# Last down product and last token block in two parts of 172 and 86 columns; factors of the other blocks by a product with ones

## The chip, the core and the metric

The kernel runs on one core of a Trainium2 chip. The metric is the device time of one execution in microseconds (us). Engines are named as the profile names them: PE is TensorE (PEld its weight loads), DVE VectorE, ACT ScalarE, POOL GpSimd, SP SyncE, which issues most DMAs.

## What is computed

One decoder layer on 1024 prompt tokens and 8 sample tokens, 1032 columns in all, model width 1024. The change touches the end of it: the channel mixer's down projection, its residual addition, and the final RMSNorm.

```python
def rmsnorm(x, g):
    xf = x.astype(jnp.float32)
    y = xf * lax.rsqrt(jnp.mean(xf * xf, axis=-1, keepdims=True) + EPS)
    return (y * g.astype(jnp.float32)).astype(x.dtype)

def sq_relu_mlp(h, w_up, w_down):
    return jnp.square(jax.nn.relu(h @ w_up)) @ w_down
...
        xp = xp + sq_relu_mlp(rmsnorm(xp, norm_mlp[l]), w_up[l], w_down[l])
...
    y_prompt = rmsnorm(xp, norm_final)
    y_sample = rmsnorm(xd, norm_final)
```

## The kernel before

Activations lie transposed: features on the 128 partitions, tokens in columns. The 1032 columns are two halves of 516, each of two chunks of QC = 258; QCOLS[2 * c + half] is a block of 258 columns. A f32 product is made of three single-pass products on values split into a high and a low part in the type fp32r (UH and UL, wh and wl), which accumulate in one PSUM bank.

The down projection is done with seven block products (Strassen's scheme, `q` in 1, 2, 6, 7, 4, 5, 3) in four groups `g` of the hidden width. A step (q, p, c) is one call of `lower`: 12 products of 128x128 weights and 258 columns for the feature tile `p` and the chunk `c`; then DVE adds the bank to the accumulator `c` of its quadrant (line 2413). The accumulators hold the residual as well. TensorE's order is pinned to the program's (`pinned`); the other engines' order is set by the tile framework's scheduler.

In the last part of group 3 (`end`), q is 5 and then 3, and the steps go chunk by chunk: n = 0 to 7 for c = 0, n = 8 to 15 for c = 1. With each addition of q 4, 2, 5 and 3 go the squares for the final norm (`squares`): ACT squares the 258 columns, DVE or POOL adds them into `ssf`; the square of the last tile of a chunk (`sqt`) is kept apart (`tails`).

The final norm of a block takes two steps, at the places that COLUMNS_AT and ROWS_AT give. `finish_columns` calls `factor_columns`: for each 86 columns (QP) of the block a product with the sums of squares as weights and a column of ones gives the sum over partitions as one column; the tail is a second term; ACT takes the square root, DVE the reciprocal (`fc`, 86x3). ACT also multiplies the accumulators by the norm's gain (line 2334). `finish_rows` calls `factor_rows`: for each 86 columns a product with the broadcast factor as weights and the identity writes the factors as a row on all partitions; DVE multiplies the accumulators by it (line 2342), and SP, for the last block ACT too, issues the output. The last block, (c, half) = (1, 1), does both after n = 15, in four multiplications of two feature tiles each.

`ones` is a 128x1 column and `onesq` a 128x128 square of ones, both f32; `factor_columns` and `factor_rows` serve the norm before the up projection as well (`norm_factor`, `norm_rows`).

Of the kernel before, what the change touches and what calls it, by code (L numbers as in the profile page):

```python
# [48 lines left out]
def decoder_step(ctx: ExitStack, tc: tile.TileContext, i: dict, o: dict):  # L49
# [1929 lines left out]
    def factor_columns(bank, sums, last, x):  # L1979
        col = bank[:QP, 300:303]  # L1980

        terms = [(y, j) for y in (sums, last) if y is not None for j in range(3)]
        for n, (y, j) in enumerate(terms):
            pinned(nc.tensor.matmul(
                col[:, j : j + 1], y[:, j * QP : j * QP + QP], ones[:, :1], start=n == 0, stop=n >= len(terms) - 3,
                skip_group_check=True))
        fc = KC.tile([QP, 3], F32, tag=f"fc{x % 2}", name=f"fc_{x}", bufs=2)
# [4 lines left out]
    def factor_rows(bank, fc):  # L1992
        for j in range(3):
            mm(bank[:, j * QP : j * QP + QP], fc[:, j : j + 1].to_broadcast([QP, P]), ident[:QP, :QP], True, True)
        return bank[:, :QC]
# [3 lines left out]
    def norm_factor(x):  # L1999
        fp = PD.tile([P, 512], F32, tag=("mk", "dt")[x % 2], name=f"rm_{x}", bufs=1)  # L2000
        FACTORS[x] = fp, factor_columns(fp, ssum[:, QCOLS[x]], None, x)
# [239 lines left out]
    with pool("acc", side="right") as AC, pool("rd", side="right") as RD, pool("w") as A, pool("w_ps", space=PSUM) as PS:  # L2241
# [22 lines left out]
        COLUMNS_AT, ROWS_AT, tails = {0: (0, 0), 3: (1, 0), 10: (0, 1), 15: (1, 1)}, {2: (0, 0), 5: (1, 0), 12: (0, 1), 15: (1, 1)}, {}  # L2264
# [39 lines left out]
        def lower(w, s, c, ps, first):  # L2304
            cq = slice(c * QC, c * QC + QC)
            for k in range(4):
                wk, wkl = w[:, k * P : k * P + P], w[:, 512 + k * P : 512 + k * P + P]
                for x, (l, r) in enumerate(((wk, s[0]), (wk, s[1]), (wkl, s[0]))):
                    pinned(nc.tensor.matmul(  # L2309
                        ps, l, r[:, k, cq], start=first and k == 0 and x == 0, stop=k == 3 and x == 2, skip_group_check=True))  # L2310

        def squares(quad, p, c, tail=False):
            cs = QCOLS[2 * c + HALF_OF[quad]]
            x = C[quad][:, p, c * QC : c * QC + QC]
# [11 lines left out]
        ends = {}  # L2326

        def finish_columns(c, half):
            fp = PS.tile([P, 512], F32, tag=f"acc{turns[0] % 8}", name=f"fin_{c}_{half}", bufs=1)
            turns[0] += 1  # L2330
            ends[c, half] = fp, factor_columns(fp, ssf[:, QCOLS[2 * c + half]], tails[c] if half else None, 4 + 2 * c + half)
# [3 lines left out]

        def finish_rows(c, half):
            cs = QCOLS[2 * c + half]
            rf = factor_rows(*ends[c, half])
            n = 2 if (c, half) == (1, 1) else 4
            for ft in range(0, 8, n):  # L2340
                y = C[((11, 21), (12, 22))[half][ft // 4]][:, ft % 4 : ft % 4 + n, c * QC : c * QC + QC]
# [285 lines left out]
```

## Time and profile before

| | |
|---|---|
| median of 3 runs | 1488.96 us (1487.69 to 1489.63) |
| the profiled execution | 1496.69 us |
| its span, first to last instruction | 1494.8 us, mean granted clock 0.995 |
| PE, PEld busy | 98%, 94% of the span |
| DVE, ACT, POOL busy | 73%, 45%, 21% |

All durations of rows come from the one profiled execution; times in them count from the span's start. An engine's busy share is an average over stages with different limits. The chain that ended last is followed back from the last instruction: at each step to what released it, or to the instruction before it on its engine.

### The profile page before, as it was taken

The numbers are of one execution on the slowest core, as the hardware profiler recorded it, in microseconds if no ns is written. First come the engines' busy times: TensorE is split into PE (matmuls) and PEld (weight loads), VectorE is DVE, ScalarE is ACT, GpSimd is POOL, SyncE is SP. The second block draws the span as 40 slices with busy tenths as digits, with TensorE's granted clock in tenths as the row PEclk, the third lists the DMA queues.
The fourth block names the chain that finished last, engine by engine and source line by source line (L and its number), as shares of the span: only waits on it lengthen the run. The fifth ranks groups of instructions, "written<-read, shape, count | busy, mean of one in ns | idle before, by whom it ended". The sixth has DMA issues, their size and how long they took to land.

```text
span 1494.8 us, 27880 instructions
## 1 busy us (share of the span) xinstructions
PE 1471.7 (98%) x10925; PEld 1401.8 (94%) x10925; DVE 1098.7 (73%) x2264; ACT 679.6 (45%) x1325; POOL 321.1 (21%) x346
## 2 busy tenths in 40 slices
PE   9999999998999999999999999999999999999997
PEld 7899779998779999989999999999999999999997
DVE  7666436887767636567886988888888879787865
ACT  7543435665552431248535643434334443343454
POOL 0035323123414311105022100000001311110380
PEclk9999999999999999999999999999999999999998
DMA  8255728213847157474582444344436774536273
GB/s 287 65 185 180 202 58 189 71 47 110 268 145 283 59 195 175 145 228 102 178 304 68 136 148 145 128 154 157 156 139 209 239 251 142 171 101 198 72 128 114
DMA packets 125238, 236.69 MB, mean 158 GB/s; under 512 B 13748, under 2 KB 76521, under 8 KB 124978
## 3 DMA queue, kind: packets, MB, share of 16 engines
q1 hardware_dynamic: 89064, 170.51, 36.0%
q0 software_dynamic: 24912, 44.80, 11.0%
q10 hardware_dynamic: 11130, 19.60, 3.5%
q8 instruction: 86, 1.41, 0.4%
q14 instruction: 46, 0.38, 0.1%
HBM read 170.25 MB, written 57.52 MB: 152 GB/s over the span
## 4 chain that ended last, share of the span: by engine, by line
PE 84%; DVE 8%; ACT 3%; issue 2%; DMA 2%; POOL 0%; ACTq 0%; another core or an unknown queue 0%; SPq 0%; DVEq 0%; POOLq 0%
PE dn L2309 19%; PE Z L2143 9%; PE qkp L75 7%; PE mq L75 6%; PE Y L2143 6%; PE X L2143 6%; PE pr_o L75 6%; PE pr_m L75 4%; PE grp L75 3%; PE sp L75 2%; PE av L75 2%; PE mv L75 1%; PE mk L75 1%; PE mpv L75 1%; PE vap_z L522 1%
## 5 line engine op out<-in xcount | busy, mean ns | idle before, releaser
L2309 PE MATMUL dn<-UH,wd 128*128 128x258 f32 x1792 | 325.1, 283 | 0.8 <-DVE c L2413 0.3
L2309 PEld LDWEIGHTS dn<-UH,wd 128*128 128x128 f32 x1792 | 277.6, 189 | 1.8 <-issue 0.8
L2309 PE MATMUL dn<-UL,wd 128*128 128x258 f32 x896 | 252.7, 282 | 0.0
L2309 PEld LDWEIGHTS dn<-UL,wd 128*128 128x128 f32 x896 | 169.0, 189 | 0.0
L2413 DVE TENSOR_TENSOR c<-c,dn 128x258 f32<-128x258 f32 x216 | 88.5, 417 | 38.2 <-PE dn L2309 35.8
L2169 ACT ACTIVATE hq<-r 128x258 f32<-128x258 f32 x128 | 53.9, 422 | 114.1 <-DVE r L2168 114.1
L2143 PE MATMUL X<-UH,wu 128*128 128x258 f32 x512 | 97.4, 282 | 0.9 <-ACT p L2194 0.9
L2143 PE MATMUL Z<-T_h,wu 128*128 128x258 f32 x512 | 98.2, 284 | 0.0
L2287 ACT CAST wd<-raw_d 128x512 fp32r<-128x512 f32 x96 | 58.8, 620 | 78.4 <-PE dn L2309 73.2
L1953 ACT CAST wu<-raw_up 128x512 fp32r<-128x512 f32 x96 | 59.2, 617 | 62.2 <-PE Z L2143 54.7
L2280 ACT CAST UH<-raw_h 128x1032 fp32r<-128x1032 f32 x56 | 58.8, 1057 | 55.0 <-PE dn L2309 27.3
L2143 PEld LDWEIGHTS X<-UH,wu 128*128 128x128 f32 x512 | 81.3, 188 | 1.1 <-ACT p L2194 1.1
L2143 PEld LDWEIGHTS Z<-T_h,wu 128*128 128x128 f32 x512 | 81.3, 189 | 0.0
L2281 DVE TENSOR_TENSOR UL<-raw_h,UH 128x1032 fp32r<-128x1032 f32 x56 | 73.4, 1311 | 9.9 <-ACT UH L2280 9.9
L2180 POOL DMA_DIRECT2D HT<-ht x32 | 17.2, 536 | 292.4 <-DVE ht L2179 291.9
L2288 DVE TENSOR_TENSOR wd<-raw_d,wd 128x512 fp32r<-128x512 f32 x96 | 72.0, 757 | 10.0 <-ACT wd L2287 9.9
L2143 PE MATMUL Z<-T_l,wu 128*128 128x258 f32 x256 | 72.3, 282 | 0.0
L2143 PE MATMUL X<-UL,wu 128*128 128x258 f32 x256 | 72.3, 282 | 0.0
L128 ACT CAST wh_u<-raw_u 128x1024 fp32r<-128x1024 f32 x43 | 44.7, 1049 | 54.2 <-PE mq L75 31.2
L1954 DVE TENSOR_TENSOR wu<-raw_up,wu 128x512 fp32r<-128x512 f32 x96 | 64.5, 684 | 3.7 <-ACT wu L1953 3.7
L129 DVE TENSOR_TENSOR wl_u<-raw_u,wh_u 128x1024 fp32r<-128x1024 f32 x39 | 51.6, 1328 | 18.3 <-ACT wh_u L128 18.1
L2301 POOL TENSOR_TENSOR raw_d<-raw_d,raw_d 128x512 f32<-128x512 f32 x16 | 22.1, 1382 | 194.5 <-DVE raw_d L2297 173.4
(598 smaller groups left out, 4718.2 us busy)
## 6 DMA issues: line engine op xcount, KB each, us to landing
raw_u<-in_wall SPq DMA_DIRECT2D x49, 512.0 KB
HT<-ht POOLq DMA_DIRECT2D x32, 516.0 KB
raw_h<-HT SPq DMA_DIRECT2D x32, 516.0 KB
raw_up<-in_wall SPq DMA_DIRECT2D x32, 512.0 KB
raw_d<-in_wall SPq DMA_DIRECT2D x32, 512.0 KB
HQ<-hq ACTq DMA_DIRECT2D x32, 387.0 KB
raw_h<-HQ SPq DMA_DIRECT2D x24, 516.0 KB
cmk<-in_cmk SPq DMA_DIRECT2D x16, 512.0 KB
```

The costliest lines, as they stand in the source:

```text
L75: pinned(nc.tensor.matmul(out, l, r, start=start, stop=stop))
L129: (lo_engine or nc.vector).tensor_sub(wl[:, :n], raw[:, :n], wh[:, :n].bitcast(F32))
L1953: nc.scalar.copy(w[:, :512], src)
L1954: nc.vector.tensor_sub(w[:, 512:], src, w[:, :512].bitcast(F32))
L2143: pinned(nc.tensor.matmul(ps, l, r[:, k, :], start=first and k == 0 and x == 0, stop=k == 3 and x == 2, skip_group_check=True))
L2169: nc.scalar.activation(h[:, PLACE[quad], :], r, AF.Square)
L2280: nc.scalar.copy(h, rv)
L2281: nc.vector.tensor_sub(l, rv, h.bitcast(F32))
L2287: nc.scalar.copy(w[:, :512], src)
L2288: nc.vector.tensor_sub(w[:, 512:], src, w[:, :512].bitcast(F32))
L2309: pinned(nc.tensor.matmul(ps, l, r[:, k, cq], start=first and k == 0 and x == 0, stop=k == 3 and x == 2, skip_group_check=True))
L2413: nc.vector.tensor_add(y, y, ps)
```

## The change

For the three earlier blocks the two steps become one, `finish_sums`: a product of the sums with the square of ones gives the sum over partitions on all partitions at once, as 128x258 (block (0, 1) needs two products, the tail's too); ACT takes the square root in PSUM, DVE the reciprocal of 258 columns into `ssf`, and `finish_rows` multiplies by `ssf` without a further product.

The last step (3, 3, 1) and the last block are cut into PARTS, 172 and 86 columns: `lower`, the addition and the square of the tail are done for one part and then for the other. After the loop `final_sums` is done for both parts, then `final_rows` for both. `factor_columns` and `factor_rows` take n = 2 or 1 instead of 3. The last block's multiplications are of four feature tiles and one part each.

```diff
+    def factor_columns(bank, sums, x, last=None):
+        n = sums.shape[-1] // QP
+        col = bank[:QP, 300 : 300 + n]
...
-        COLUMNS_AT, ROWS_AT, tails = {0: (0, 0), 3: (1, 0), 10: (0, 1), 15: (1, 1)}, {2: (0, 0), 5: (1, 0), 12: (0, 1), 15: (1, 1)}, {}
+        SUMS_AT, ROWS_AT, tails = {0: (0, 0), 3: (1, 0), 10: (0, 1)}, {2: (0, 0), 5: (1, 0), 12: (0, 1)}, {}
...
+        WHOLE, PARTS = slice(0, QC), (slice(0, 2 * QP), slice(2 * QP, QC))
+
+        def lower(w, s, c, ps, first, part):
+            cq = slice(c * QC + part.start, c * QC + part.stop)
...
-                sq = A.tile([P, QC], F32, tag="sqt", name=f"sqt_{c}", bufs=2)
+                sq = A.tile([P, QC], F32, tag="sqt", name=f"sqt_{c}_{part.start}", bufs=3)[:, part]
...
+        def finish_sums(c, half):
+            f = acc_bank(f"fin_{c}_{half}")
+            y = ssf[:, QCOLS[2 * c + half]]
+            mm(f, onesq, y, True, not half)
+            if half:
+                mm(f, onesq, tails[c, 0], False, True)
+            nc.scalar.activation(f, f, AF.Sqrt, scale=1.0 / D, bias=epsc)
+            nc.vector.reciprocal(y, f)
             for ft in range(8):
                 y = C[((11, 21), (12, 22))[half][ft // 4]][:, ft % 4, c * QC : c * QC + QC]
                 nc.scalar.activation(y, y, AF.Copy, scale=g_fin[:, ft : ft + 1])
...
+        def final_sums(part):
+            fp = PS.tile([P, 512], F32, tag=f"acc{turns[0] % 8}", name=f"fin_1_1_{part.start}", bufs=1)
+            turns[0] += 1
+            y = ssf[:, QCOLS[3]][:, part]
+            ends[part.start] = fp, factor_columns(fp, y, 4 + part.start, tails[1, part.start])
+            for ft in (3,) if part.start else (0, 1, 2, 3, 4, 5, 6, 7):
+                y = final_y(ft, 1, part if ft == 3 else WHOLE)
+                nc.scalar.activation(y, y, AF.Copy, scale=g_fin[:, ft : ft + 1])
+
+        def final_rows(part):
+            rf = factor_rows(*ends[part.start])
+            cs = slice(HALF + QC + part.start, HALF + QC + part.stop)
+            for ft in (4, 0):
+                y = final_y(ft, 4, part)
+                nc.vector.tensor_mul(y, y, rf.unsqueeze(1).to_broadcast([P, 4, part.stop - part.start]))
+                (nc.scalar if ft else nc.sync).dma_start(
+                    o["yT"][ft * P : (ft + 4) * P, cs].rearrange("(f p) c -> p f c", p=P), y)
...
-                steps = [(q, p, c) for q in qs for p in ps_ for c in range(2)]
+                steps = [(q, p, c, WHOLE) for q in qs for p in ps_ for c in range(2)]
                 if end:
-                    steps = [(q, p, c) for c in range(2) for q in qs for p in ps_]
-                for n, (q, p, c) in enumerate(steps):
+                    steps = [(q, p, c, WHOLE) for c in range(2) for q in qs for p in ps_]
+                    steps[-1:] = [(*steps[-1][:3], x) for x in PARTS]
+                for n, (q, p, c, part) in enumerate(steps):
...
+        for part in PARTS:
+            final_sums(part)
+        for part in PARTS:
+            final_rows(part)
```

The order of instructions at the end of TensorE's queue, before (`fin_1` is the bank of the last block's factors, `dn_5_3_1` that of the last product):

```order
L2309 MATMUL dn_5_3_1_17235<-UH,wd_3_3_17150 128x258 x2
L2309 MATMUL dn_5_3_1_17235<-UL,wd_3_3_17150 128x258
L2309 MATMUL dn_5_3_1_17235<-UH,wd_3_3_17150 128x258
L1984 MATMUL fin_1_17322<-ones,ssumf 86x1 x3
L1984 MATMUL fin_1_17322<-ones,sqt_17320 86x1 x3
L75 MATMUL fin_1_17322<-ident,fc_17329 128x86 x3
```

and in the changed kernel, from the last products of the second part on:

```order
L2313 MATMUL dn_5_3_1_17218<-UH,wd_3_3_17138 128x86 x2
L2313 MATMUL dn_5_3_1_17218<-UL,wd_3_3_17138 128x86
L2313 MATMUL dn_5_3_1_17218<-UH,wd_3_3_17138 128x86
L1985 MATMUL fin_1_0_17317<-ones,ssumf 86x1 x2
L1985 MATMUL fin_1_0_17317<-ones,sqt_0_17300 86x1 x2
L1985 MATMUL fin_1_172_17333<-ones,ssumf 86x1
L1985 MATMUL fin_1_172_17333<-ones,sqt_172_17315 86x1
L75 MATMUL fin_1_0_17317<-ident,fc_17322 128x86 x2
L75 MATMUL fin_1_172_17333<-ident,fc_17336 128x86
```

The column products of both parts stand behind the products of both; the row products of the first part stand behind the columns of the second.

The end of ACT's queue in the changed kernel (`sqt_0` and `sqt_172` are the squares of the two parts' last tile, `c_13388` the accumulators of quadrant 12, features 0 to 511, `c_13387` of quadrant 22, `fc` the factors):

```order
L2321 ACTIVATE sqt_0_17300<-c_13388 128x172
L2354 ACTIVATE c_13388<-c_13388,g_fin 128x172
L1989 ACTIVATE fc_17322<-fin_1_0_17317,epsc 86x2
L2321 ACTIVATE sqt_172_17315<-c_13388 128x86
L2354 ACTIVATE c_13388<-c_13388,g_fin 128x86
L1989 ACTIVATE fc_17336<-fin_1_172_17333,epsc 86x1
L2362 DMA out_yT<-c_13387 128x4x172
L2362 DMA out_yT<-c_13387 128x4x86
```

The square of the second part stands behind the square root of the first part's factors, which reads what TensorE's columns wrote.

The end of DVE's queue in the changed kernel:

```order
L2442 TENSOR_TENSOR c_13388<-c_13388,dn_5_3_1_17218 128x172
L2442 TENSOR_TENSOR c_13388<-c_13388,dn_5_3_1_17218 128x86
L1990 RECIPROCAL fc_17322<-fc_17322 86x2
L2361 TENSOR_TENSOR c_13387<-c_13387,fin_1_0_17317 128x4x172
L1990 RECIPROCAL fc_17336<-fc_17336 86x1
L2361 TENSOR_TENSOR c_13388<-c_13388,fin_1_0_17317 128x4x172
L2361 TENSOR_TENSOR c_13387<-c_13387,fin_1_172_17333 128x4x86
L2361 TENSOR_TENSOR c_13388<-c_13388,fin_1_172_17333 128x4x86
```

The two additions of the last product come first, then one reciprocal for each part and four multiplications of four feature tiles.

## Rows read from the trace of the kernel before

**Rows 1.** The page: busy time of TensorE; shares of the chain that ended last.

```profile
PE 1471.7 (98%) x10925; PEld 1401.8 (94%) x10925; DVE 1098.7 (73%) x2264; ACT 679.6 (45%) x1325; POOL 321.1 (21%) x346
...
PE 84%; DVE 8%; ACT 3%; issue 2%; DMA 2%; POOL 0%; ACTq 0%; another core or an unknown queue 0%; SPq 0%; DVEq 0%; POOLq 0%
```

**Rows 2.** The chain that ended last, from 1456 us: start, us, what.

```profile
1458.44 0.39 PE fin L1984 x6
...
1461.81 0.64 PE fin L75 x6
...
1464.31 2.97 PE dn L2309 x24
...
1467.92 7.24 PE dn L2309 x60
1475.16 0.85 PE fin L1984 x12
...
1478.99 0.65 PE fin L75 x6
...
1482.37 0.34 DVE c L2413
...
1483.72 0.43 DVE ssumf L2324
...
1487.78 0.69 DVE c L2342
```

**Rows 3.** Timeline: start, us, engine, line, operation, count [idle before <-releaser].

```profile
1473.75 0.42 DVE L2413 TENSOR_TENSOR c<-c,dn 128x258 f32<-128x258 f32 x1 [1.00 <-PE dn L2309]
...
1483.70 0.28 PE L2309 MATMUL dn<-UH,wd 128*128 128x258 f32 x1
1484.20 0.62 PE L1984 MATMUL fin<-ones,ssumf 128*86 128x1 f32 x6 [0.22 <-DVE ssumf L2324]
...
1485.64 0.26 ACT L1988 ACTIVATE fc<-fin,epsc 86x3 f32<-86x3 f32 x1 [0.17 <-PE fin L1984]
```

**Rows 4.** Windows: us, busy time (instructions) by engine, PEclk, DMA share, GB/s.

```profile
1484.00:1486.00 2.00, 1.24 (x12) 1.07 (x12) 0.54 (x3) 1.48 (x4) 0.00 (x0) 1.00 0.60 164
1486.00:1488.00 2.00, 1.58 (x6) 1.36 (x6) 0.33 (x2) 0.00 (x0) 0.00 (x0) 0.51 0.03 9
...
1490.00:1492.00 2.00, 0.00 (x0) 0.00 (x0) 0.28 (x1) 0.00 (x0) 0.00 (x0) 0.50 1.03 345
```

**Rows 5.** Timeline of TensorE elsewhere: plain-f32 products in a row.

```profile
146.96 1.10 PE L75 MATMUL sc<-qblk,kT 128*128 128x256 f32 x4
...
324.32 1.84 PE L75 MATMUL ct<-ones,sq 128*128 128x1 f32 x16
...
833.67 1.47 PE L75 MATMUL rm<-ident,fc 86*128 86x86 f32 x12
```

**Rows 6.** Groups by form: out<-in, shapes xcount | busy us, mean ns | idle before.

```profile
L2309 PE MATMUL dn<-UH,wd 128*128 128x258 f32 x1792 | 325.1, 283 | 0.8 <-DVE c L2413 0.3 <-ACT c L2410 0.3
...
L2309 PEld LDWEIGHTS dn<-UH,wd 128*128 128x128 f32 x1792 | 277.6, 189 | 1.8 <-issue 0.8 <-ACT c L2410 0.5 <-DVE c L2413 0.3
...
L545 PEld LDWEIGHTS vrp_d<-wl_vr,UD 128*8 128x8 f32 x16 | 1.4, 88 | 0.0
...
L2342 DVE TENSOR_TENSOR c<-c,fin 128x1032 f32<-128x1032 f32 x6 | 7.3, 1225 | 0.4 <-PE fin L75 0.4
...
L1013 DVE RECIPROCAL mn<-sm 128x1 f32<-128x1 f32 x32 | 5.1, 159 | 2.4 <-ACT e L1006 1.8 <-issue 0.5
...
L1067 DVE RECIPROCAL c<-sm 128x8 f32<-128x8 f32 x4 | 0.8, 188 | 0.0
```

**Rows 7.** DMA queues, 1488 to 1495: packets, MB, share of 16 engines.

```profile
q1 hardware_dynamic: 544, 0.53, 22.7%
q10 hardware_dynamic: 544, 0.53, 22.0%
```

**Rows 8.** The same, 238.1 to 239.0, 512 bytes a packet.

```profile
q1 hardware_dynamic: 432, 0.22, 104.7%
```

More of the change, by code (lines that the diff above doesn't have):

```diff
@@ L1977, in decoder_step @@
     QP = QC // 3
[L1979 to L1983, printed above, removed]
+    def factor_columns(bank, sums, x, last=None):
+        n = sums.shape[-1] // QP
+        col = bank[:QP, 300 : 300 + n]
+        terms = [(y, j) for y in (sums, last) if y is not None for j in range(n)]
+        for m, (y, j) in enumerate(terms):
             pinned(nc.tensor.matmul(
-                col[:, j : j + 1], y[:, j * QP : j * QP + QP], ones[:, :1], start=n == 0, stop=n >= len(terms) - 3,
+                col[:, j : j + 1], y[:, j * QP : j * QP + QP], ones[:, :1], start=m == 0, stop=m >= len(terms) - n,
                 skip_group_check=True))
-        fc = KC.tile([QP, 3], F32, tag=f"fc{x % 2}", name=f"fc_{x}", bufs=2)
+        fc = KC.tile([QP, 3], F32, tag=f"fc{x % 2}", name=f"fc_{x}", bufs=2)[:, :n]
         nc.scalar.activation(fc, col, AF.Sqrt, scale=1.0 / D, bias=epsc[:QP])
@@ L1992, in factor_rows @@
     def factor_rows(bank, fc):
-        for j in range(3):
+        n = fc.shape[-1]
+        for j in range(n):
             mm(bank[:, j * QP : j * QP + QP], fc[:, j : j + 1].to_broadcast([QP, P]), ident[:QP, :QP], True, True)
-        return bank[:, :QC]
+        return bank[:, : n * QP]
     FACTORS = {}
@@ L2334, in finish_columns, with final_y @@
                 nc.scalar.activation(y, y, AF.Copy, scale=g_fin[:, ft : ft + 1])
+        ends = {}
+        def final_y(ft, n, part):
+            return C[(12, 22)[ft // 4]][:, ft % 4 : ft % 4 + n, QC + part.start : QC + part.stop]
+        def final_sums(part):
[14 more added lines that the diff above has]
+                    o["yT"][ft * P : (ft + 4) * P, cs].rearrange("(f p) c -> p f c", p=P), y)
         def finish_rows(c, half):
             cs = QCOLS[2 * c + half]
[L2338 to L2341, printed above, removed]
-                nc.vector.tensor_mul(y, y, rf.unsqueeze(1).to_broadcast([P, n, QC]))
-                (nc.scalar if n == 2 and ft % 4 else nc.sync).dma_start(
-                    o["yT"][ft * P : (ft + n) * P, cs].rearrange("(f p) c -> p f c", p=P), y)
+            rf = ssf[:, cs]
+            for ft in range(0, 8, 4):
+                y = C[((11, 21), (12, 22))[half][ft // 4]][:, ft % 4 : ft % 4 + 4, c * QC : c * QC + QC]
+                nc.vector.tensor_mul(y, y, rf.unsqueeze(1).to_broadcast([P, 4, QC]))
+                nc.sync.dma_start(o["yT"][ft * P : (ft + 4) * P, cs].rearrange("(f p) c -> p f c", p=P), y)
         pin[0] = True
@@ L2419, in decoder_step @@
                         if q in (2, 4, 5, 3):
[L2420 removed]
+                            tail = squares(INTO[q], p, c, (q, p) == (3, 3), part)
                         if tail is not None:
[L2422 to L2424 removed]
+                            tails[c, part.start] = tail
+                        if end and n in SUMS_AT:
+                            finish_sums(*SUMS_AT[n])
                         if end and n in ROWS_AT:
                             finish_rows(*ROWS_AT[n])
+        for part in PARTS:
+            final_sums(part)
+        for part in PARTS:
+            final_rows(part)
         pin[0] = False
```

24 lines of the change are left out of this document (7 added, 17 removed).

## The prediction

> **What bounds the kernel now.** I read the page first. TensorE is busy for 98% of the span and carries 84% of the chain that ended last [rows 1], so an edit on its queue counts while that queue is full. The chain in order of time says until when [rows 2]: from 1458 on it is down products (dn) with small norm products (fin) between them, nothing else; after 1479.64 it passes to VectorE (DVE) and ScalarE (ACT), but TensorE has no idle time before the first fin of the last group, which starts at 1484.20, 0.22 of it waited [rows 3]. From there TensorE is no longer the limit. The end is a relay: last addition, square, column products, square root, reciprocal, row products, multiplications, output transfers [rows 3]. The windows show two more things [rows 4]: the granted clock is 1.00 to 1486 and 0.51 (the 1.2 GHz level) after it, when TensorE had been busy for only 1.24 of the last 2.00 us; and the transfers fill the 16 DMA engines from 1490 to 1492 (share 1.03). So there are two regions: a full TensorE queue up to the last product, and a serial tail of 11 us.
>
> The sum below is made against the profiled execution (1496.69 us, span 1494.8, 1.9 around it). It is 7.7 us above the median of the three runs, 1488.96; I take the same number of us off both.
>
> **TensorE before the last product: 1.9 us less.** In the last group of the loop the three earlier blocks lose their column and row products. The chain gives their share: columns 0.39 twice and 0.85, rows 0.64, 0.63 and 0.65, together 3.55 [rows 2] (of the two 0.39 one stands there, of the rows the first and the last). In their place come four products of 128x258 in plain f32 (one, one, two). None of that shape is in the trace. The nearest is sc, 128x256 in plain f32: four records, two products, in 1.10 us [rows 5], so 0.55 each at most, and about 0.45 where the next product hides the last record's tail. I take 0.47, four are 1.9. That leaves 1.65. Each switch between dn and fin costs besides: 24 dn records between two fin groups take 2.97 [rows 2], 24 at the pitch of 0.12 (60 in 7.24) take 2.88, so 0.1 a switch, and three fin groups fewer are 0.3. Bounds 1.35 and 2.2; I take 1.9. The last product, whose 12th record starts at 1483.70 [rows 3] and whose first therefore started near 1482.38, then begins at 1480.45.
>
> The new square roots (128x258 on ACT, about as long as the addition of that size, 0.42, against 0.26 now [rows 3]) lie in ACT's idle time. The three new reciprocals of 258 columns are DVE work. Small ones take 159 ns for one column and 188 for eight [rows 6], 4 ns a column, so 1.2 us each (below: 0.42 like an addition; above: 2.0, twice the slope less the start). DVE has room between the additions, which wait for products (1.00 ahead of the one at 1473.75 [rows 3]); I count nothing. What covers it is the last product: DVE must only have the first part's addition and ACT its square done before TensorE reaches the columns that read it.
>
> **The last product: 1.25 us more.** 12 products of 258 columns take 12 x 0.12 = 1.44. Now there are 12 of 172 and 12 of 86, each with its own weight load. A load's record grows from 88 ns at 8 columns to 189 at 128 [rows 6], 0.84 ns a column, so 128 columns occupy the loader for about 0.11. The 1-column products of ct, with the same 128 columns of weights and next to nothing to stream, say the same: 16 in 1.84, 0.112 each without the tail [rows 5]. So I take 0.112 for every one of the 24, whatever its columns: 2.69. Below: time by columns alone, 0.12 x 172/258 and 0.12 x 86/258, 1.44 in all. Above: the plain-f32 price, in the rivals. It ends at 1483.15 instead of 1483.82.
>
> **The tail to the first multiplication: 2.15 us earlier.** TensorE's order puts both parts' products ahead of any columns, so the first part's norm does not start under the second part's products; only its addition and square do. Before, the sums stood 1.44 us after the end of the last but one addition (1482.71 to 1484.15) [rows 2]; that addition now ends near 1481.15, so the sums stand by 1482.6, the 172 columns are added by 1482.9 and squared by 1483.25. Their columns are reached at 1483.5, after four others: in time. The first part's eight column records (0.08 each: six take 0.62 with the last one's tail [rows 3]) end at 1483.9, their result at 1484.05. Square root to 1484.31. Now comes what is queued behind what: on ACT the second part's square stands behind this square root, so it ends near 1484.6, and on TensorE the first part's row products stand behind the columns that read that square. These end at 1484.8, so the four row records run to 1485.4 at 0.112 each (rm: 12 in 1.47 at full clock [rows 5]; to 1485.9 at the half clock, where six took 1.58 [rows 4]). The reciprocal is done meanwhile. The first multiplication is now 4x172 columns, between 516 in 0.69 [rows 2] and 1032 in 1.22 [rows 6], so 0.87, and ends at 1486.32; before, the first one ended at 1488.48 [rows 2]. The second part's factors hide under it.
>
> **The output transfers: 0.8 us more.** After the first multiplication the DMA engines set the pace [rows 4]: two queues with 544 packets each, at 22.7% and 22.0% of 16 engines over 7 us [rows 7], are 46 ns a packet, 64 data packets an engine, 3.0 us. Bytes stay the same, packets double: 64 of 688 bytes and 64 of 344 an engine. Below: by bytes, nothing more. Above: the 512-byte packets of [rows 8] take 35 ns (432 at 104.7% of 0.9 us); on that line 688 bytes are 39 and 344 bytes 31, 4.5 us, 1.5 more. I take 0.8. The last multiplication and its issue end near 1488.2, ahead of their turn.
>
> **Sum.** -2.15 + 0.8 = -1.35, rounded -1.4: the profiled execution at 1495.3, the runs at 1487.6, 0.09% faster. With the bounds of these terms (0.3 and 0.55 on TensorE, 0.5 for the half clock, 0.8 and 0.7 on the transfers) 1486.5 to 1489.3. About 0.2% (2.98 us: below 1485.98, above 1491.94) is what a measurement of this kernel can tell from no change.
>
> **Rivals.**
> First, products by columns (0.15). If a weight load hides fully even under 86 columns, the last product stays 1.44 and ends at 1481.9; then the first part's square (1483.25) binds the columns, whose result comes at 1483.75 instead of 1484.05: 0.3 more, 1487.3. Against it stand the ct rows [rows 5]. The Trainium skill ("TensorE: Matmul & The Clock Gate", Back-to-back issue gap) gives columns / 2.4 GHz + 2.5 ns for an isolated gap, 74 and 38 ns here, 1.35 us in all; the trace does not bear that out for loads of 128 f32 columns.
>
> Second, ending slower (0.25): the single-pass products (fp32r, one record each, where a plain f32 product has two) fall to the plain-f32 price. The down products all have 258 columns [rows 6], and no row shows a single-pass product of fewer than 256. Place: the 24 products at the end. Price: rm, 86 columns, 12 records or six products in 1.47, 0.225 each; sc at 256 about 0.45; so 172 near 0.32. 12 x (0.32 + 0.225) = 6.5, 3.8 above the 2.69 taken: -1.4 + 3.8 = +2.4, 1491.4. It decides from 24 products in 4.1 us, 0.17 each. For it: nothing in the trace, but nothing excludes it either. Against it: the load of such a product has the same length as that of a wide one.
>
> Third, the narrow output packets (0.08). The 86-column part writes 344-byte runs. If each costs two moves, 64 x 31 ns come on top: +2.0, +0.6 in all, 1489.6. The Trainium skill ("DMA: Bandwidth & Descriptors", Specifications) asks for 512 bytes and names a read-modify-write below; no run here shows a write of that size.
>
> Fourth, DVE becomes the bound (0.04): it decides when the last of the three reciprocals takes some 2.0 us, for its lateness then eats the 0.25 us by which the first part's square is in time and the wait ahead of the last but one addition. At 3 us the end moves by 1.0, 1488.6.
>
> My forecast has 0.48.
>
> **How the numbers follow.** The time is that of the likeliest case, 1487.6. The range goes from the low bound of that case with the first rival's 0.3 on top, 1486.2, to just above the second rival, 1491.5; it leaves out the dearer half of the second rival and the tails of the others, some 0.18. Faster by over 0.2% needs the low bounds of several terms at once: 0.07. Slower by over 0.2% needs the second rival at a price over 0.6 us above mine: 0.07. Within 0.2%: 0.86.
>
> **What would show it.** In the changed kernel's chain: four plain-f32 fin products of 128x258 (eight records) and no row products before the last one; the last product starting some 1.9 us nearer the loop's start. In the timeline: the pitch of the 172- and 86-column records, 0.112 for both if I am right, 0.08 and 0.04 for the first rival, 0.2 to 0.3 for the second. The second square behind the first square root on ACT, and the row products behind it on TensorE. Reciprocals of 258 columns near 1.2 us. The last transfers at 39 and 31 ns a packet or less. The forecast is wrong if the last product takes over 4 us, or if the span ends over 7.8 us after the first multiplication (1488.48 to 1494.8, 6.3, before).

## The result, and the profile after

The changed kernel takes 1490.57 us (median of 14 runs, 1488.20 to 1495.01), the kernel before 1487.88 beside it (14 runs, 1486.10 to 1492.29). The ratio is 1.0016, 95% interval 1.0008 to 1.0023: slower by 2.4 us. Timed again beside other runs it is 1.0017 (1.0008 to 1.0026). In one version below (whole rows out) one run took 2882 us and is left out of the ratio. The forecast was 0.09% faster; the time lies within the range that was given, but the sign is the other one.

The profiled execution took 1491.64 us, its span is 1489.9. First the page of the changed kernel, the two lines that answer to [rows 1]:

```profile
PE 1468.3 (99%) x10903; PEld 1398.7 (94%) x10903; DVE 1101.1 (74%) x2266; ACT 678.1 (46%) x1328; POOL 321.5 (22%) x346
...
PE 86%; DVE 7%; ACT 3%; issue 2%; DMA 1%; POOL 0%; ACTq 0%; SPq 0%; DVEq 0%; POOLq 0%
```

Shares say nothing here: TensorE was busy for 3.4 us less and the time rose. The chain that ended last does, in order of time (start, us, what), against [rows 2]:

```profile
1451.12 0.44 PE fin L75 x2
...
1456.32 10.11 PE dn L2313 x84
...
1466.45 0.43 DVE c L2442
...
1467.84 1.65 issue
1469.49 0.36 DVE c L2442
1469.85 1.14 DVE c L2370
1470.99 0.34 DVE ssumf L2328
1471.33 0.33 DVE c L2442
1471.66 1.15 DVE c L2370
...
1474.93 0.25 DVE c L2442
...
1475.22 1.83 PE dn L2313 x12
1477.05 1.12 PE fin L1985 x8
...
1478.19 0.26 ACT fc L1989
1478.45 0.17 ACT sqt L2321
...
1478.67 0.45 PE fin L1985 x2
1479.12 1.01 PE fin L75 x4
...
1480.15 0.87 DVE c L2361
```

Before, the chain stayed on TensorE down to 1479.64, some 4 us ahead of the last product's end. Now it leaves TensorE at 1466.4 and runs through DVE: the third reciprocal (of its 1.77 us, 1.65 stand as "issue"), two multiplications, additions. Then it comes back to TensorE for only 12 records, those of the second part, which begin at 1475.22 right behind an addition. Behind that the relay is the one predicted: second square behind the first square root on ACT, row products behind the second part's columns. The three reciprocals as a group by form (busy us, mean ns):

```profile
L2337 DVE RECIPROCAL ssumf<-fin 128x258 f32<-128x258 f32 x3 | 5.3, 1770 | 0.5 <-ACT fin L2336 0.5
```

The timeline of the same kernel (start, us, engine, line, operation, count, idle time before it and what ended that) and the waits of TensorE from 1455 to 1490 say what the 12 records waited for:

```profile
1473.96 0.96 DVE L2328 TENSOR_TENSOR ssumf<-ssumf,sqc_f 128x258 f32<-128x258 f32 x2 [0.15 <-ACT sqc_f L2327]
...
1474.07 0.27 PE L2313 MATMUL dn<-UH,wd 128*128 128x172 f32 x1
...
1474.84 0.33 DVE L2442 TENSOR_TENSOR c<-c,dn 128x172 f32<-128x172 f32 x1
...
1475.22 0.31 PE L2313 MATMUL dn<-UH,wd 128*128 128x86 f32 x1 [0.88 <-DVE c L2442]
```

```profile
PE fin L75 <- DVE fc L1990: 1.0, 1, 1.0
PE dn L2313 <- DVE c L2442: 0.9, 1, 0.9
```

The first part's products end at 1474.34. DVE is still in two additions to the sums of squares and adds the first part only at 1474.84; TensorE waits 0.88 us, to the end of that addition, before it starts the second part. The windows (busy time, granted clock, DMA share, GB/s) show the rest:

```profile
1474.00:1476.00 2.00, 1.12 (x11) 0.96 (x10) 1.06 (x3) 1.83 (x5) 0.00 (x0) 1.00 0.70 225
1476.00:1478.00 2.00, 2.00 (x15) 2.00 (x15) 0.24 (x1) 0.02 (x1) 0.00 (x0) 0.58 0.00 0
...
1482.00:1483.00 1.00, 0.00 (x0) 0.00 (x0) 0.84 (x2) 0.00 (x0) 0.00 (x0) 0.50 1.03 323
1483.00:1484.00 1.00, 0.00 (x0) 0.00 (x0) 0.00 (x0) 0.00 (x0) 0.00 (x0) 0.50 1.07 259
1484.00:1485.00 1.00, 0.00 (x0) 0.00 (x0) 0.00 (x0) 0.00 (x0) 0.00 (x0) 0.50 1.21 177
```

In this execution the clock falls to its half level (0.50, 1.2 GHz) at 1476.3, after TensorE had been busy for 1.12 of 2.00 us, and the last of the second part's products, all column products and all row products run at that level. At the end the DMA engines are full (a share over 1 means packets that overlap in an engine) while their rate drops from 323 to 177 GB/s; before, they moved 345 [rows 4]. Their queues from 1481 to 1488, to be held against [rows 7]:

```profile
q1 hardware_dynamic: 1056, 0.53, 43.0%
q10 hardware_dynamic: 1056, 0.53, 35.4%
```

Together that is 78.4% of 16 engines for 7 us, where it was 44.7% for the same bytes.

To compare executions whose earlier parts differ by a few us, I count from the start of the first down product of the last group; the changes begin behind it. Before that product stands at 1456.84, after at 1449.53 of the span. The positions (us) are worked out from each timeline in this way, one execution of each kernel; the last column is the end less the first multiplication's start. The clock fell to its half level at 29.2 before, at 26.8 to 27.1 in after and in the two kernels with two banks, and at 28.4 or later in the others.

| kernel | last product starts | its last record | first multiplication | end | the difference |
|---|---|---|---|---|---|
| before | 25.53 | 26.86 | 30.94 | 38.00 | 7.06 |
| after | 23.35 | 27.11 | 30.62 | 40.35 | 9.73 |
| after, second profile | 23.35 | 26.95 | 29.19 | 38.43 | 9.24 |
| product with ones alone | 23.35 | 24.68 | 28.38 | 35.40 | 7.02 |
| split alone | 25.53 | 28.85 | 31.10 | 40.83 | 9.73 |
| parts in output alone | 23.35 | 24.68 | 28.38 | 37.78 | 9.40 |
| two banks | 23.35 | 25.83 | 28.97 | 38.38 | 9.41 |
| sums behind | 23.35 | 26.50 | 28.74 | 38.15 | 9.41 |
| wait filled | 23.35 | 26.94 | 29.18 | 38.39 | 9.21 |
| whole rows out | 23.35 | 26.95 | 29.19 | 37.07 | 7.88 |
| two banks, sums behind, whole rows | 23.35 | 25.83 | 28.88 | 36.56 | 7.68 |

So the last product does begin 2.18 us sooner. All of that and more is given back in two places: between its start and the first multiplication, and behind the first multiplication.

### The profile page after: what moved, and what is told of

Same layout as the page of the kernel before. It is cut to its first block, busy times and chain, and to the rows that moved or that the text cites. A ratio compares the mean times of both kernels' runs of the same rounds, so it can differ in the third digit from the quotient of the medians.

```text
span 1489.9 us, 27845 instructions
## 1 busy us (share of the span) xinstructions
PE 1468.3 (99%) x10903; PEld 1398.7 (94%) x10903; DVE 1101.1 (74%) x2266; ACT 678.1 (46%) x1328; POOL 321.5 (22%) x346
## 4 chain that ended last, share of the span: by engine, by line
PE 86%; DVE 7%; ACT 3%; issue 2%; DMA 1%; POOL 0%; ACTq 0%; SPq 0%; DVEq 0%; POOLq 0%
PE dn L2313 21%; PE Z L2145 9%; PE qkp L75 7%; PE mq L75 6%; PE Y L2145 6%; PE X L2145 6%; PE pr_o L75 5%; PE pr_m L75 4%; PE grp L75 3%; PE sp L75 2%; PE av L75 2%; PE mv L75 2%; PE mk L75 1%; PE mpv L75 1%; PE vap_z L522 1%
## 5 line engine op out<-in xcount | busy, mean ns | idle before, releaser
L2313 PE MATMUL dn<-UH,wd 128*128 128x258 f32 (+1 forms) x1800 | 325.5, 283 | 1.0 <-DVE c L2442 0.9
L2442 DVE TENSOR_TENSOR c<-c,dn 128x258 f32<-128x258 f32 (+1 forms) x217 | 88.6, 416 | 36.3 <-PE dn L2313 34.1
L75 PE MATMUL qkp<-UH,wh_u 128*128 128x344 f32 x192 | 62.9, 327 | 0.1
```

What stands on the lines that cost most here:

```text
L75: pinned(nc.tensor.matmul(out, l, r, start=start, stop=stop))
L2313: pinned(nc.tensor.matmul(ps[:, part], l, r[:, k, cq], start=first and k == 0 and x == 0, stop=k == 3 and x == 2, skip_group_check=True))
L2442: nc.vector.tensor_add(y, y, ps)
```

## The experiments

Three theories were set against each other: W, the wait of the second part's products for the first part's addition; D, DVE made late by the three reciprocals; P, the output in runs of 688 and 344 bytes. Ratios are to the kernel before, timed beside each.

**The product with ones alone.** The three earlier blocks as in the change; nothing of the last product or block is split.

```
-        WHOLE, PARTS = slice(0, QC), (slice(0, 2 * QP), slice(2 * QP, QC))
+        WHOLE = slice(0, QC)
+        PARTS = (WHOLE,)
...
+            for ft in range(0, 8, 2):
...
+                (nc.scalar if ft % 4 else nc.sync).dma_start(
...
-                    steps[-1:] = [(*steps[-1][:3], x) for x in PARTS]
```

> Only the product with ones for the three earlier blocks; the last product, the last block's norm and its output transfers in one piece as before the change. Three theories of the 2.4 us by which the changed kernel came out slower. W: the second part's products wait for the first part's addition, since they write the accumulator that it reads (0.9 us idle, after which the granted clock falls), so the split gives back what the fewer norm products gained. D: the three reciprocals of 258 columns (1.77 us each instead of the 1.2 assumed) put DVE behind, so that the additions come late. P: the output in runs of 688 and 344 bytes takes longer than in runs of 1032. By W and P the last product starts 2.2 us nearer the first down product of the last group than in the kernel before, all that follows moves with it, and the time is 1.7 to 2.2 us below the kernel before. By D the last addition starts more than 0.5 us after the last product's end and the time is less than 1.2 us below the kernel before.

1486.14 us (12 runs), ratio 0.9987 (0.9979 to 0.9996): 1.9 us faster (0.6 to 3.1). Its last addition starts at 24.99, 0.03 after the last product's end, although DVE carries the same three reciprocals. By its position, and by the median, D as it was put is refuted for the product with ones, and this half of the change is worth its whole forecast. Its timeline shows a smaller cost on DVE all the same:

```profile
1476.82 0.42 DVE L2442 TENSOR_TENSOR c<-c,dn 128x258 f32<-128x258 f32 x1
1477.16 0.42 DVE L2329 TENSOR_TENSOR ssumf<-ssumf,sqc_f 128x258 f32<-128x258 f32 x1
...
1477.63 0.62 PE L1985 MATMUL fin<-ones,ssumf 128*86 128x1 f32 x6 [0.85 <-DVE ssumf L2329]
```

One addition to the sums now stands behind the last addition, and the column products wait 0.85 us for it, where they waited 0.22 before [rows 3]. The columns of the last square come 2.94 us after the last product's start, 2.62 before. Whether the reciprocals or the scheduler's choice put it there is not shown.

**The split alone.** The other half: the three earlier blocks get the old column and row products and small reciprocals back.

```
         def finish_sums(c, half):
-            f = acc_bank(f"fin_{c}_{half}")
...
-            nc.vector.reciprocal(y, f)
+            fp = PS.tile([P, 512], F32, tag=f"acc{turns[0] % 8}", name=f"fin_{c}_{half}", bufs=1)
+            turns[0] += 1
+            ends[c, half] = fp, factor_columns(fp, ssf[:, QCOLS[2 * c + half]], 4 + 2 * c + half, tails[c, 0] if half else None)
...
-            rf = ssf[:, cs]
+            rf = factor_rows(*ends[c, half])
```

> The split alone: the changed kernel with the column and row products and the small reciprocals of the kernel before for the three earlier blocks. If the two edits add up: the last product starts near 25.5 (from the start of the first down product of the last group) as in the kernel before, 2.2 later than in the changed kernel; DVE is not late, so the first part's addition starts 1.5 after the last product's start instead of 1.97; the time is 1.3 to 2.2 us above the changed kernel, 3.5 to 5 above the kernel before. If the reciprocals' load on DVE is what makes the split dear (D), the split alone costs nothing and the time is within 1 us of the kernel before.

1491.48 us (6 runs), ratio 1.0032 (1.0020 to 1.0045). The halves add up: 1.0032 x 0.9987 = 1.0019, and 1.0016 was measured. The split costs 4.8 us (3.0 to 6.7) and the product with ones brings 1.9. Without large reciprocals the first part's addition starts 1.69 after the last product's start (27.22), not the 1.5 that I expected: the sums' additions are ahead of it there too, and TensorE waits 0.6 us.

**Two banks.** Each part of the last product accumulates in a bank of its own; the product that shared the bank is added by one more DVE addition.

```
+                    own = end and (p, c) == (3, 1)
-                    if q == qs[0]:
+                    if q == qs[0] or own:
...
-start=first and k == 0 and x == 0
+start=(first or own) and k == 0 and x == 0
...
+                    if own and q == 5:
+                        y = C[12][:, p, cq]
+                        nc.vector.tensor_add(y, y, ps)
```

> The changed kernel, but the two parts of the last product accumulate in two banks of their own; the earlier product that shared the bank is added to the second sum by one more addition on DVE (0.33 to 0.42 us, well before). W: no wait ahead of the second part's products, 24 records at a pitch of 0.11, the last one 1.2 us earlier and the clock at 1.00 to their end; the first multiplication 1.2 to 1.8 us earlier, the time 1.2 to 1.8 us below the changed kernel. D: DVE, and not the bank, sets the pace; the first part's addition is another 0.3 us later and the time is within 0.5 us of the changed kernel, or above it.

1489.08 us (12 runs), ratio 1.0010 (1.0001 to 1.0018). The wait for DVE is gone. The waits of TensorE from 1455 to 1481 in this kernel, complete:

```profile
PE fin L75 <- DVE fc L1990: 1.0, 1, 1.0
PE fin L1985 <- ACT sqt L2321: 0.4, 1, 0.4
```

The last record comes at 25.83, 1.28 sooner than after and 1.12 sooner than in its second profile, with 24 records at 0.11. In positions W is shown: it is the shared accumulator that holds the second part back. In the built program the first of the second part's products carries a wait for DVE, which is gone here; whether the chip would bear that wait's absence in one bank was not tried. The time fell by some 0.9 us, less than the 1.2 expected, and the intervals of the two kernels overlap. The extra addition and DVE's queue put the first part's addition at 25.75, 0.93 after its product's end, which is D at work once the wait is gone. The clock fell at 27.1 here, so the first part's row products took 1.14 us where the second profile of the changed kernel has 0.66; the first multiplications, 28.97 and 29.19, differ by less than the wait for that reason too.

**Sums behind.** DVE's two additions to the sums of squares go behind the first part's addition.

```
+            if quad == 12 and c == 1 and p in (1, 2):
+                late.append((ssf[:, cs], sq))
+                return
...
+                    if late and (p, c) == (3, 1) and q == 3:
+                        with tc.issue_after(nc.cur_bb.bb.instructions[-1]):
+                            for x, sq in late:
+                                nc.vector.tensor_add(x, x, sq)
```

> The changed kernel, but DVE's two additions to the sums of squares that stand ahead of the first part's addition (0.43 us each) come behind it. Positions are counted from the start of the first down product of the last group. D (DVE is late when the first part's products end): the first part's addition starts at 24.9 instead of 25.32, the last record of the last product moves from 27.11 to 26.7 or less, and the time falls by 0.4 us, or by up to 1.8 where the shorter wait keeps the clock up. W alone (the wait is the addition's own length and its two hand-overs): addition and last record stay within 0.1 of where they are.

1489.06 us (11 runs), ratio 1.0016 (1.0007 to 1.0025). The timeline of this kernel:

```profile
1473.01 0.34 DVE L2445 TENSOR_TENSOR c<-c,dn 128x172 f32<-128x172 f32 x1 [0.57 <-PE dn L2313]
...
1473.41 0.31 PE L2313 MATMUL dn<-UH,wd 128*128 128x86 f32 x1 [0.43 <-DVE c L2445]
```

Now DVE waits for TensorE (0.57), and TensorE for the addition alone (0.43 where it was 0.88): addition at 24.85, last record at 26.50. D's positions hold: 0.45 of the wait is DVE's queue and 0.43 is the addition with its hand-overs, which no order of DVE's work removes. The time does not show the 0.45: the interval is 2.7 us wide.

**Third block's multiplications on GpSimd.** An attempt to relieve DVE in another way.

```
-                nc.vector.tensor_mul(y, y, rf.unsqueeze(1).to_broadcast([P, 4, QC]))
+                (nc.gpsimd if (c, half) == (0, 1) else nc.vector).tensor_mul(y, y, rf.unsqueeze(1).to_broadcast([P, 4, QC]))
```

> The changed kernel, but the two multiplications of 4 x 258 columns of the third block (1.22 us each on DVE) run on GpSimd, so that DVE is not behind when the first part's products end. D: the first part's addition follows its product at once, 0.45 us earlier than now, the wait ahead of the second part's products shrinks to about 0.45 us, the clock stays up some 0.5 us longer, and the time falls by 0.5 to 1.2 us. W alone: the wait is set by the addition's own length and its two hand-overs (0.9 us), the time stays within 0.3 us of the changed kernel.

Neither: 1493.69 us (5 runs), ratio 1.0038 (1.0025 to 1.0051). The timeline, DVE and POOL:

```profile
1470.27 4.98 POOL L2370 TENSOR_TENSOR c<-c,ssumf 128x1032 f32<-128x1032 f32 x2 [18.03 <-DVE ssumf L2337]
...
1470.81 0.42 DVE L2442 TENSOR_TENSOR c<-c,dn 128x258 f32<-128x258 f32 x1 [0.34 <-PE dn L2313]
1471.15 4.38 DVE L2328 TENSOR_TENSOR ssumf<-ssumf,sqc_f 128x258 f32<-128x258 f32 x2
1475.45 0.41 DVE L2442 TENSOR_TENSOR c<-c,dn 128x258 f32<-128x258 f32 x1
```

Two additions of 0.43 us stretch to 4.38 while GpSimd multiplies. DVE was not relieved but held up, by some 2.7 us, and TensorE waited 3.4 us for its additions. It shows, the wrong way round, that a late DVE does reach the end of this kernel. The clock stayed at 1.00 through that wait and fell only at 29.4.

**The wait filled.** Eight more products between the two parts.

```
+                    if end and part.start:
+                        spare = acc_bank("spare")
+                        for x in range(8):
+                            pinned(nc.tensor.matmul(spare, W[q, p][:, :P], S[q][0][:, 0, QC : 2 * QC], start=True, stop=True))
```

> The changed kernel with eight more products of 258 columns into a bank that nobody reads, between the two parts of the last product, so that TensorE is busy in the wait for the first part's addition. The extra products are left unused. If the wait is what lets the granted clock fall: it stays at 1.00 to 28.5 or later (from the start of the first down product of the last group) instead of 26.8, the second part's products keep the pitch of 0.11, the first multiplication starts near 29.3 instead of 30.62, and the time is 0.6 to 1.4 us below the changed kernel. If the clock falls for another reason, it falls near 26.8 as before, and the time is 0 to 0.3 us above the changed kernel.

1490.13 us (11 runs), ratio 1.0021 (1.0012 to 1.0030): no gain in time, and not told apart from the changed kernel. In the profile the clock stays at 1.00 to 29.9 and the first multiplication starts at 29.18, both as expected of the first reading; but the next run takes that profile's weight away.

**The changed kernel once more.** No edit.

> The changed kernel itself, timed and profiled once more beside the others. If the clock's fall in the wait is a matter of the execution and not of the program: about half of the runs show a mean granted clock of 0.995 or less and lie some 2 us or more above the others; in the profile the clock falls either near 26.8 (from the start of the first down product of the last group; first multiplication at 30.6) or after 29 (first multiplication at 29.2, end at 38.2 to 38.9). If it falls every time: all runs at 0.995 or less.

1490.88 us (11 runs), ratio 1.0017. The windows of this second profile of the same program:

```profile
1474.00:1476.00 2.00, 1.46 (x14) 1.46 (x14) 0.49 (x2) 1.17 (x3) 0.00 (x0) 1.00 0.31 105
1476.00:1478.00 2.00, 1.64 (x17) 1.40 (x16) 0.41 (x2) 1.04 (x4) 0.00 (x0) 1.00 0.00 0
1478.00:1480.00 2.00, 0.72 (x2) 0.50 (x2) 1.92 (x4) 0.00 (x0) 0.00 (x0) 0.63 0.04 14
```

Here the clock falls at 29.7, with nothing filled, and the first multiplication is 1.43 us earlier (29.19 against 30.62). When the clock falls in the relay is a matter of the execution. The longest wait of all, 3.4 us with the multiplications on GpSimd, did not bring it down either. The expectation of two clear groups did not come out: of the 25 timed runs in both batches eight (seven of the first fourteen, one of these eleven) show a mean clock of 0.995 or less, with a median of 1491.3, the other 17 have 1489.9. The mean is also a blunt sign, for short stretches at the half level far ahead of the end lower it too: the profile of the filled run has one from 780.4, that of before two, from 356.2 and 786.3. Beside the filled run, whose eleven are all at 0.996 or more and no faster, the clock's share of the loss in the median stays open; one execution shows what it can be, 1.43 us.

**Whole rows out.** The last block's output in two transfers of 4 x 258 columns, each behind the second part's multiplication.

```
+                if part.start:
+                    (nc.scalar if ft else nc.sync).dma_start(
+                        o["yT"][ft * P : (ft + 4) * P, HALF + QC : T].rearrange("(f p) c -> p f c", p=P), final_y(ft, 4, WHOLE))
```

> The changed kernel, but the last block leaves in two transfers of 4 x 258 columns (runs of 1032 bytes), each issued after the second part's multiplication. P: the packets start some 1.4 us later, but take 3.2 us instead of 5.0 and are complete sooner after the last one; the end comes 0.7 to 1.2 us earlier than in the changed kernel. If the size of the packets is not the cost (W and D alone), the end comes 0.3 to 1.4 us later than in the changed kernel.

1488.66 us (11 runs), ratio 0.9999 (0.9990 to 1.0008). 2.5 us below the changed kernel by the ratios. Its first multiplication starts where that of the changed kernel's second profile does (29.19 in both). The first transfer is issued 1.4 us later, at 31.50 against 30.09, and the end comes 1.36 earlier, at 37.07 against 38.43. P holds.

**Parts in the output alone.** The kernel without the split; only its last multiplications and transfers are cut to 4 x 172 and 4 x 86 columns.

```
+            for part in (slice(0, 2 * QP), slice(2 * QP, QC)):
...
+                for ft in (4, 0):
+                    y = final_y(ft, 4, part)
```

> The kernel without the split (product with ones only), but the last block's multiplications and output transfers in the changed kernel's parts, 4 x 172 and 4 x 86 columns. P: with the same start of the first multiplication, the packets of 688 and 344 bytes take 4.7 to 5.0 us instead of 3.2 to 3.4, their completion half a us longer, and the time is 1.2 to 2.4 us above the kernel without the split. If the packets are not the cost: within 0.5 us of it.

1488.75 us (11 runs), ratio 1.0008 (0.9999 to 1.0017), against 0.9987 without the parts: 2.1 thousandths, 3 us. With the first multiplication at 28.38 in both, the end moves from 35.40 to 37.78. Nothing ahead of the last multiplications differs, and the same bytes take 2.4 us more. The windows, first of the kernel without the parts, from the first full microsecond of its transfers:

```profile
1482.00:1483.00 1.00, 0.00 (x0) 0.00 (x0) 0.70 (x2) 0.00 (x0) 0.00 (x0) 0.50 1.03 331
1483.00:1484.00 1.00, 0.00 (x0) 0.00 (x0) 0.00 (x0) 0.00 (x0) 0.00 (x0) 0.50 1.05 354
```

and of the kernel with them:

```profile
1479.00:1480.00 1.00, 0.00 (x0) 0.00 (x0) 0.29 (x1) 0.00 (x0) 0.00 (x0) 0.50 1.06 314
1480.00:1481.00 1.00, 0.00 (x0) 0.00 (x0) 0.00 (x0) 0.00 (x0) 0.00 (x0) 0.50 1.08 258
1481.00:1482.00 1.00, 0.00 (x0) 0.00 (x0) 0.00 (x0) 0.00 (x0) 0.00 (x0) 0.50 1.20 177
1482.00:1483.00 1.00, 0.00 (x0) 0.00 (x0) 0.00 (x0) 0.00 (x0) 0.00 (x0) 0.50 1.35 175
```

The engines are full in both. With twice the packets they take 4.65 us from first to last instead of 3.26, and from the last packet to the end it is 2.9 us instead of 2.1.

**The same with 129 and 129 columns.** Twice the packets again, but all of 516 bytes.

```
-            for part in (slice(0, 2 * QP), slice(2 * QP, QC)):
+            for part in (slice(0, QC // 2), slice(QC // 2, QC)):
```

> The kernel without the split of the product, whose multiplications and outputs go in two parts of 129 columns each (2048 packets of 516 bytes) where the run before it had 172 and 86. If the number of packets is the cost: the packets take 4.4 to 5.0 us as with 172 and 86 columns, the end stays within 0.4 us of that run. If packets under 512 bytes are the cost: the packets take 3.3 to 4.0 us, complete sooner, and the end comes 0.8 to 1.8 us earlier than in that run.

1489.42 us (11 runs), ratio 1.0012 (1.0002 to 1.0021). The queues from 1479 to 1486:

```profile
DMA packets 2112, 1.06 MB, mean 151 GB/s; under 512 B 64, under 2 KB 2112, under 8 KB 2112
...
q10 hardware_dynamic: 1056, 0.53, 42.5%
q1 hardware_dynamic: 1056, 0.53, 34.0%
```

No data packet is under 512 bytes (the 64 are small ones that before has too), and it is as slow: 4.9 us of packets against 4.65, 76.5% of the engines against 73.3% in the run before it, end at 37.41 against 37.78. So it is not the packets under 512 bytes; the cost goes with twice the packets for the same bytes. No run sets their number apart from their size and start addresses.

**All three mended.** Two banks, sums behind, whole rows in four transfers of 2 x 258 columns.

```
+            rfs = [factor_rows(*ends[part.start]) for part in PARTS]
+            for ft in range(0, 8, 2):
+                for part, rf in zip(PARTS, rfs):
...
+                    o["yT"][ft * P : (ft + 2) * P, HALF + QC : T].rearrange("(f p) c -> p f c", p=P), final_y(ft, 2, WHOLE))
```

> The changed kernel without what W, D and P name: two banks for the two parts, the additions to the sums behind the first part's addition, and the output in four transfers of 2 x 258 columns, each behind the multiplications of both parts. If these three are the whole loss: the first multiplication starts at 27.7 to 28.0 (from the start of the first down product of the last group), the end comes at 34.7 to 35.2, and the time is 0.2 to 0.7 us below the kernel without the split. If the split itself costs more (24 products of 0.11 us for 12 of 0.12, and the two norms behind each other): the first multiplication at 28.4 or later and the time equal to the kernel without the split, or above it.

1486.62 us (11 runs), ratio 0.9999 (0.9990 to 1.0008); the kernel without the split has 0.9987. So a split without W, D and P is still no gain: its first multiplication, at 28.88, comes no sooner than 28.38. The 24 narrow records put the last one at 25.83 instead of 24.68, and the two norms stand behind each other on ACT and TensorE. In this execution the clock fell at 27.1, with no wait ahead of the second part: the first part's row products took 1.14 us, 0.66 in the changed kernel's second profile, and that is nearly all of the 0.5. And the output starts later: the first transfer, which now waits for both parts' multiplications, is issued 1.80 us after the start of the first multiplication, 0.76 without the split, and 7.68 us pass to the end instead of 7.02.

**A smaller first multiplication.** The kernel without the split, with one tile instead of two in the first multiplication.

```
+            for x, (ft, n) in enumerate(((0, 1), (1, 1), (2, 2), (4, 2), (6, 2))):
```

> The kernel without the split, with the last block's first multiplication cut to one tile of 258 columns instead of two, so that the first output transfer can start sooner (five transfers instead of four, same packets). If the end is set by the first packet and 3.2 us of packets: the first packet and the end come 0.25 to 0.35 us earlier than without the cut, the best time of all. If the last multiplication or the last issue sets it: the end stays where it was or comes up to 0.3 us later.

1486.47 us (11 runs), ratio 0.9990 (0.9981 to 0.9999): not told apart from 0.9987. In its profile the clock fell at 27.1 and the first multiplication came at 29.07 instead of 28.38, so the end, 35.48 against 35.40, doesn't decide either. No version came out better than the product with ones alone.

## Why the prediction was wrong, point by point

**TensorE before the last product: right.** 1.9 us were forecast, 2.18 measured. Four products of 128x258 in plain f32 cost less than 0.47 each: the chain has 0.44 for a single one (two records, at 1451.12), so 1.76 in all by that row.

**The last product: the first step that failed.** The prediction put all 24 products in a row and let it end at 1483.15, earlier than before. The pitch was right, 0.11 for both widths, so neither the first rival (by columns) nor the second (plain-f32 price) happened; that the second's time, 1491.4, lies near the measured one is chance. But the second part's products don't follow. They write the accumulator whose other columns the first part's addition reads, and TensorE waits until DVE is done: last record at 26.95 instead of 25.83 in executions with the same clock, 1.12 us. I had looked for what waits behind each instruction on ACT and on TensorE's small products, and not asked the first question of a split: do the two parts share anything. The Trainium skill has the rule ("PSUM — Partial Sum Buffer", PSUM bank collisions raise a hardware error): two engines may not touch one bank and quadrant at once, whatever the columns, so accesses are to be guarded by bank and not by address. The program waits as the rule asks, 0.88 us ahead of the second part with one bank and not at all with two; that an error would come without the wait no run here shows. The rule would have given a rival on the slower side. The prediction's sign of being wrong, a last product of over 4 us, came in the first profile (4.18 from its start to its end) and nearly in the second (3.89).

**DVE: hidden, as forecast, but only in one half.** The reciprocals take 1.77 us each, not 1.2 (bounds 0.42 and 2.0). Costed at nothing, they are nearly free with an unsplit last product, whose addition is on time, and a split one uses up the slack: the first part's addition starts 0.50 after its product's end. Of the 0.88 us that TensorE waits, 0.45 are DVE's queue, as the sums put behind show; 0.28 go with the reciprocals (the wait is 0.60 without them, in the split alone). The prediction had that addition late enough: it put it behind the sums and let it end 2.45 us after the last product's start, where 2.30 were measured. What it lacked, in the fourth rival too, is that TensorE waits for it.

**The tail to the first multiplication.** Forecast 2.15 earlier at its end. With the clock up it ends at 30.06 against 31.63 (it is 0.87 long, as taken): 1.57 earlier; where the clock falls in the relay, at 31.49, 0.14 earlier. The order of the relay was the forecast one. The forecast had set row products at the full level against before's at the half level; that level is a matter of the execution (four records in 0.66 us or in 1.13), so up to 0.5 of the 2.15 hung on it.

**The output transfers: the second step, and the dearer one, mis-sized.** Forecast +0.8, at most +1.5. Measured 2.4 with all else equal. Whole rows alone brought the runs back by 2.5 us, two banks alone by some 0.9. The prediction's other sign of being wrong came as well: the span ends 8.4 and 8.9 us after the first multiplication, not within 7.8. The bound was built on time per packet in another stretch and on the packets alone. The first 512 packets of 688 bytes did take 35 ns, under the 39 forecast; then the rate sank, the next 512 took 44 to 55 ns and those of 344 bytes 32 to 45, where 31 was forecast. The completion behind the last packet, 0.8 us of the 2.4, wasn't in the sum. The third rival had the direction and the wrong reason: runs of 516 bytes cost as much (4.9 us of packets against 4.65), so a threshold at 512 bytes does not decide here. The Trainium skill ("DMA: Bandwidth & Descriptors", Specifications) states one, 512 bytes for the full rate; these runs do not bear it out as the cause.

**The sum with the measured terms.** Ends of the first multiplication 1.57 earlier, behind it 8.37 instead of 6.37 (end less end of the first multiplication): +0.43 by the second profile, +2.35 by the first. The runs say +2.4 to +2.5. The profile of before may itself be a late one: its row products ran at the half level, 1.60 us where the kernel without the split has 0.91. Its mean clock, 0.995 where 80 of 90 later runs of the same kernel have 0.997 or 0.998, does not show that, for its two short stretches far ahead of the end take 0.002 of it. But in every row of the table the version's runs stand higher against those of before than its end does against 38.00, by 0.0 to 2.7 us. Against an execution of before with row products at the full level the sums would be about +1.1 and +3.0, and the runs would lie between; no second profile of before was taken, so how often that is the case stays open.

## What to carry to other kernels

Before work is cut into parts so that they overlap, list what the parts still share: here an accumulator's bank made the second part wait for the first one's reader, and the cut then added hand-overs instead of hiding them. Price a last transfer that fills the DMA engines by its packets, and by its completion behind them: here twice the packets for the same bytes cost 2.4 us, more than the 2.18 by which the last product started sooner. And test the halves of a change apart: one of these was worth 1.9 us and the other cost 4.8.

## What the runs showed of the hardware

- A reciprocal of 128x258 on DVE takes 1.77 us, 6.9 ns a column, where the small ones suggested 4 [rows 6].
- Full DMA engines moved 331 to 354 GB/s in packets of 1032 bytes, and about 175 in the later half of a stream of 688 and 344, which began at 314: the first packets don't show the price.
- While GpSimd multiplied (4.98 us), two DVE additions with both operands in SBUF took 4.38 us instead of 0.86, and one that reads the accumulator took its 0.42. The Trainium skill describes it ("SBUF — State Buffer", SBUF: two separate sides): the two engines share a port pair that one holds for its whole instruction. The trace agrees: the two additions end at 1472.98 and 1475.53, each 0.28 us behind the end of one of the two GpSimd multiplications.
- The same program had its clock fall at 26.8 in one execution and at 29.7 in another (from the start of the first down product of the last group); the first multiplications lie 1.43 us apart.
